# Two queue edits in a one-core attention/pooling block: low parts of weights ahead of sums and forms on VectorE, and one more panel in the last attention-branch run

## The chip, the cores and the metric

The kernel runs on one core of a Trainium2 chip. The metric is the device time of one execution in microseconds (us). Two programs that differ by less than about 0.2% can't be told apart by this kernel's measurement; the three runs below lie within 0.07%.

## The reference

One layer on 512 tokens of width 2048, all in float32. The parts that matter here, cut from the reference:

```python
h = rms_norm(x, norm_mix)
z = h @ w_in                                    # q, k, v, u, gate_a, gate_b
y_a = chunked_rel_attention(q, k, v, rel_bias)  # width 1024
y_b = multiscale_pool(u, pool_w, pool_scale)    # width 1024
merged = sigmoid(gate_a) * (y_a @ w_branch_a) + sigmoid(gate_b) * (y_b @ w_branch_b)
x = x + merged @ w_out
x = x + swiglu(rms_norm(x, norm_ffn), w_gate_up, w_down)
return rms_norm(x, norm_final)
```

## The kernel before

**Split numbers.** A float32 matmul is made of three matmuls of a reduced float32 form (fp32r). Each operand is split into a high part (a copy that rounds, on ScalarE) and a low part (the operand minus its high part, on VectorE); TensorE adds low x high, high x high and high x low in the same bank of its accumulator memory.

**First part: panels.** `panel` multiplies a panel of 256 weight columns with all tokens. Weights come in *staged units* (512 KB `raw` loads; `hi` and `lo` are their parts). A *gate panel* ("g") takes the 2048 rows of `w_in`, a *branch panel* ("y") the 1024 rows of `w_branch_a` or `w_branch_b`, so a branch panel has 2 staged units of 24 matmuls for each of two output columns. `a_order` lists the last 16 panels: g0, y0, g1, y1, ... and then, for the last `N_TAIL` values of i, all gate panels ahead of all branch panels. A branch panel's results (`m_dram`, two tiles of 128 columns for each panel) go to memory by GpSimd's queue.

**Second part: jobs.** The output projection, the gate/up projection and the down projection run as 38 *jobs*. A job takes a 1024 x 1024 block of weights and computes it by a scheme with 7 products in place of 8 (P1, P5, P6, P3, P7, P2, P4, in this order). Each product has two *units* of 12 matmuls (128 x 512), so a job has 14 units (the last two jobs, with half the rows, 7 each); I number units through all jobs (job 21 begins with unit 294) and call a unit by its number, its weight parts `hiw303`, `low303`. Three things feed a job:

- *Weights.* Quarter blocks `r11`, `r12`, `r21`, `r22` are loaded by SyncE's queue (`load2_to`). For P5, P6, P7 and P4 VectorE first adds one quarter to another in place (`t_to`, lines 842 to 848: the *running sums*). Then ScalarE makes the high part `hiw` (`hi2_to`, line 856) and VectorE the low part `low` (`lo2_to`, line 864). There are `SPLIT` = 3 buffers of each, so the parts of unit i+3 may only be written when unit i is done.
- *Forms.* The activations' side of each product ("forms", `fP1` to `fP7`, each with a high and a low part) is made from a block of 512 activations, `half`. `build_forms` is a generator, one product for each step; for four products (P5, P6, P3, P7) VectorE first makes a sum `s` (the *make*, lines 729 to 732), then ScalarE the high part (line 737), and in the next step VectorE the low part (line 740 or 742):

```python
for p, src, sign, make in plan:
    if make:
        make()
    hi, lo = forms[p][:, prs, 0], forms[p][:, prs, 1]
    nc.scalar.activation(hi, src, AF.Copy, scale=float(sign))
    yield
    if sign > 0:
        tt(lo, src, hi.bitcast(F32), op=ALU.subtract)
```

- *Results.* At the end of a product ScalarE copies an accumulator (lines 899, 904, 909) or VectorE adds one to an *output sum* (lines 911, 916, 922, 926). In gate/up jobs of the second half, `hidden` turns results into the next activations: ScalarE's Silu (line 1017, waits for an output sum), VectorE's product (line 1020), and transposes on TensorE.

**What sets the order.** Every engine works off its own queue in the order in which the Python code issues. `step()` runs all active generators (forms, `hidden`, attention) by one step; panels call it after each output column of a staged unit, jobs after each unit. `run_job` issues for unit i: the running sum of unit i+3, `hiw` of unit i+2, the 12 matmuls, the product's end if there is one, `step()`, and last `low` of unit i+2. After the last branch panel `drain()` calls `step()` until no generator is left; the forms of the first job (`build_merged(fo, 0)`) start behind the last gate panel and need `m_dram` 0 to 7, of branch panels 0 to 3, only.

Of the kernel before, what the change touches and what calls it, by code (L numbers as in the profile page):

```python
# [28 lines left out]
SPLIT = 3  # L29
# [8 lines left out]
N_C = 6  # L38
LOAD_AHEAD = 7
PAD_CONST, PAD_CONST1, PAD_SLOTS, PAD_RIGHT = 96, 56, 80, 120  # L40
N_TAIL = 3

T_BY_DMA = False

# [2 lines left out]
def hybrid_block_kernel(  # L47
# [81 lines left out]
    def add_panel(w, nk, c0, r0=0, cuts=None):  # L129
        k = 0  # L130
        for n in cuts or [KU] * (nk // KU):
            units.append((rows(w, r0 + k * P, n, c0, CU), n))
            k += n
        assert k == nk
# [4 lines left out]
    def staged(kind, i, dt=F32R):  # L139
        return stage.tile([P, KU * CU], dt, tag=kind, name=f"{kind}{i}", bufs=AHEAD if kind == "raw" else SPLIT)  # L140
# [49 lines left out]
    def step():  # L190
        now, later[:] = list(later), []
        for fn in now:
            fn()
        since[0] += 1
        if waiting and since[0] >= spacing[0]:
            active.append(waiting.popleft())
            since[0] = 0
        for g in list(active):
            if next(g, "end") == "end":
                active.remove(g)  # L200
        for n in behind:
            lo_to(n)
            load_to(n + AHEAD)
        behind.clear()
# [60 lines left out]
    for what, i in b_order:  # L265
        if what == "g":
            add_panel(w_in, KD, GB + i * CU)
        else:
            add_panel(w_branch_b, KB, i * CU)
    a_order = [x for i in range(n_blk - N_TAIL) for x in (("g", i), ("y", i))]  # L270
    a_order += [(what, i) for what in "gy" for i in range(n_blk - N_TAIL, n_blk)]
    for what, i in a_order:
# [482 lines left out]
    def ctile():  # L755
        serial[0] += 1
        return cpools[-1].tile([P, 2, 512], F32, tag="c", name=f"c_{serial[0]}")

    def bank2(kind):
        serial[0] += 1  # L760
        if kind == "a":
            return ps2.tile([P, 512], F32, tag="a", name=f"psa_{serial[0]}", bufs=2)
        return ps2.tile([P, 2, 512], F32, tag=kind, name=f"ps{kind}_{serial[0]}", bufs=2 if kind == "x" else 1)
# [49 lines left out]
    def wide(t):  # L813
        return t.rearrange("p (k c) -> p k c", c=512)

    def load2_to(n):
        while loads and loads[0][0] <= n:
            _, j, q, h = loads.pop(0)
            t = rawtile(j, q, h)
            s, f = {"11": (0, 0), "12": (0, 1), "21": (1, 0), "22": (1, 1), "t1": (0, 0), "t3": (1, 1)}[q]  # L820
            nc.sync.dma_start(wide(t), j.quarter(s, f, h))
            if q[0] == "t":
                nc.gpsimd.dma_start(wide(t), j.quarter(0, 1, h), accum_op=ALU.add)
# [3 lines left out]
    def source(i):  # L827
        j, p, h = wunits[i]
        a = ("t1" if T_BY_DMA else "11") if p in ("P5", "P6") else "11"
        q = {"P1": "11", "P5": a, "P6": a, "P3": "22", "P7": "t3" if T_BY_DMA else "12", "P2": "21", "P4": "21"}[p]  # L830
        return j.raw[q, h]

    def t_to(n):

        while st2["t"] < min(n, len(wunits)):
            i = st2["t"]
            j, p, h = wunits[i]
            r = {q: t for (q, hh), t in j.raw.items() if hh == h}
            run = r.get("t1", r.get("11"))
            lo2_to(i - j.nh + 1)  # L840
            if p == "P5" and not T_BY_DMA:
                nc.vector.tensor_tensor(run, run, r["12"], op=ALU.add)
            elif p == "P6":
                nc.vector.tensor_tensor(run, run, r["22"], op=ALU.add)
            elif p == "P7" and not T_BY_DMA:
                nc.vector.tensor_tensor(r["12"], r["12"], r["22"], op=ALU.add)
            elif p == "P4":
                nc.vector.tensor_tensor(r["21"], r["21"], run, op=ALU.add)
            st2["t"] += 1

    def hi2_to(n):
        while st2["hi"] < min(n, len(wunits)):
            i = st2["hi"]
            t_to(i + 1)
            hi_t[-1 - i] = staged("hi", f"w{i}")
            nc.scalar.activation(hi_t[-1 - i], source(i), AF.Copy)  # L856
            st2["hi"] += 1

    def lo2_to(n):
        while st2["lo"] < min(n, len(wunits)):  # L860
            i = st2["lo"]
            hi2_to(i + 1)
            lo_t[-1 - i] = staged("lo", f"w{i}")
            nc.vector.tensor_tensor(lo_t[-1 - i], source(i), hi_t[-1 - i].bitcast(F32), op=ALU.subtract)  # L864
            st2["lo"] += 1
# [3 lines left out]
    def run_job(j):  # L869
        forms = j.forms  # L870
        X = Y = Z = None
        a = p5 = u2 = None
        for n, p in enumerate(PRODUCTS):
            if p == "P1":
                X = ps = bank2("x")
            elif p == "P5":
                Y = ps = bank2("y")
            elif p == "P2":
                Z = ps = bank2("y")
            else:  # L880
                ps = Y if p == "P3" else X
            for h in range(j.nh):
                i = j.base + n * j.nh + h
                load2_to(i + LOAD_AHEAD)
                t_to(i + SPLIT + 1)
                hi2_to(i + SPLIT)
                hi, lo = wide(hi_t.pop(-1 - i)), wide(lo_t.pop(-1 - i))
                for t in range(2):
                    for k in range(2):
                        fh, fl = forms[p][:, 2 * h + k, 0, TOK[t]], forms[p][:, 2 * h + k, 1, TOK[t]]  # L890
                        first = p in ("P1", "P5", "P2") and h == 0 and k == 0
                        last = h == j.nh - 1 and k == 1
                        mm(ps[:, t], fh, lo[:, k], start=first, stop=False, skip_group_check=True)  # L893
                        mm(ps[:, t], fh, hi[:, k], start=False, stop=False, skip_group_check=True)  # L894
                        mm(ps[:, t], fl, hi[:, k], start=False, stop=last, skip_group_check=True)  # L895
                if h == j.nh - 1:
                    if p == "P1":
                        a = ctile()
                        nc.scalar.activation(a, X, AF.Copy)
                        if j.acc:  # L900
                            nc.gpsimd.dma_start(a, j.acc["11"], accum_op=ALU.add)
                    elif p == "P5":
                        p5 = ctile()
                        nc.scalar.activation(p5, Y, AF.Copy, scale=-1.0)
                        if j.acc:
                            nc.gpsimd.dma_start(p5, j.acc["22"], accum_op=ALU.add)
                    elif p == "P6":
                        u2 = ctile()
                        nc.scalar.activation(u2, X, AF.Copy, scale=-1.0)
                    elif p == "P3":  # L910
                        nc.vector.tensor_tensor(u2, u2, Y, op=ALU.subtract)
                        if j.acc:
                            nc.gpsimd.dma_start(u2, j.acc["12"], accum_op=ALU.add)
                        j.done("12", u2)
                    elif p == "P7":
                        nc.vector.tensor_tensor(p5, p5, X, op=ALU.subtract)
                        j.done("22", p5)
                        if j.acc:
                            c21 = ctile()
                            nc.sync.dma_start(c21, j.acc["21"])  # L920
                    elif p == "P2":
                        nc.vector.tensor_tensor(a, a, Z, op=ALU.add)
                        j.done("11", a)
                    elif p == "P4":
                        if j.acc:
                            nc.vector.tensor_tensor(c21, c21, X, op=ALU.add)
                        else:
                            c21 = ctile()
                            nc.scalar.activation(c21, X, AF.Copy)
                        j.done("21", c21)  # L930
                step()
                lo2_to(i + SPLIT)


    def tok2(ap, th, c0):
# [279 lines left out]
```

## Time and profile before

| | us |
|---|---|
| median of 3 runs | 2540.54 (2540.34 to 2541.96) |
| the profiled execution | 2541.46 |
| its span, first to last instruction | 2539.5 |
| TensorE busy with matmuls | 2455.2 (97%) |
| VectorE busy | 1732.6 (68%) |
| ScalarE busy | 1163.4 (46%) |
| GpSimd busy | 151.3 (6%) |
| mean granted TensorE clock | 0.992 |

The profiled execution's time is 2.0 us longer than its span. A busy share is a mean over the whole span: an engine with 68% can still be the one that is waited for in one stage.

### The profile page before, as it was taken

What the parts mean: (1) busy time and instruction counts of PE and PEld (TensorE: products, weight loads), DVE (VectorE), ACT (ScalarE), POOL (GpSimd) and SP (SyncE); (2) the same over time, 40 slices, a digit from 0 to 9 for tenths busy, and PEclk for the clock granted to TensorE, in tenths of its full rate; (3) what the DMA queues carried; (4) which work ended last, traced back from release to release, by engine and by line L of the source; (5) the groups of instructions that cost most, each with busy time, mean ns of one, the idle gap of its engine ahead of it and who ended that gap; (6) DMA issues with size and microseconds to landing.
All of it is one profiled execution on the core that took longest, in us unless ns stands there. A gap on an engine that the chain in (4) does not pass through costs nothing.

```text
span 2539.5 us, 29049 instructions
## 1 busy us (share of the span) xinstructions
PE 2455.2 (97%) x11221; PEld 2002.9 (79%) x11221; DVE 1732.6 (68%) x1996; ACT 1163.4 (46%) x1499; POOL 151.3 (6%) x242
## 2 busy tenths in 40 slices
PE   9999999999999998999999999999999999999995
PEld 7888888888888887777788888877878778787773
DVE  6445556533343327978877777888897888879885
ACT  5444443322232224466545445555554555555554
POOL 0000000000000000110000000000000001000014
PEclk9999999999999999999999999999999999999997
DMA  5322222323333336664443543645645646637374
GB/s 175 96 86 78 86 92 85 94 92 100 94 101 115 107 106 199 187 211 136 179 163 141 195 156 146 203 117 167 161 145 144 171 133 165 182 104 203 100 214 118
DMA packets 203146, 352.20 MB, mean 139 GB/s; under 512 B 11304, under 2 KB 95856, under 8 KB 202880
## 3 DMA queue, kind: packets, MB, share of 16 engines
q1 hardware_dynamic: 177760, 263.76, 30.9%
q0 software_dynamic: 24096, 84.49, 14.2%
q8 instruction: 88, 1.44, 0.2%
q10 hardware_dynamic: 1152, 2.10, 0.2%
q14 instruction: 50, 0.41, 0.0%
HBM read 289.44 MB, written 60.86 MB: 138 GB/s over the span
## 4 chain that ended last, share of the span: by engine, by line
PE 86%; DVE 8%; issue 3%; ACT 2%; DMA 1%; ACTq 0%; SPq 0%; POOL 0%; DVEq 0%; POOLq 0%
PE psd L211 10%; PE psd L212 10%; PE psd L213 10%; PE psx L893 8%; PE psx L894 8%; PE psx L895 8%; PE psy L893 7%; PE psy L895 7%; PE psy L894 7%; DVE low L864 3%; PE psd L423 1%; DVE fP L740 1%; PE psd L425 1%; PE psd L424 1%; ACT hiw L856 1%
## 5 line engine op out<-in xcount | busy, mean ns | idle before, releaser
L864 DVE TENSOR_TENSOR low<-r,hiw 128x1024 fp32r<-128x1024 f32 x518 | 630.4, 1225 | 133.7 <-ACT hiw L856 131.4
L856 ACT ACTIVATE hiw<-r 128x1024 fp32r<-128x1024 f32 x518 | 546.5, 1057 | 377.0 <-PE psx L895 157.6
L893 PE MATMUL psx<-low,fP 128*128 128x512 f32 x1184 | 471.7, 398 | 29.7 <-DVE low L864 25.2
L894 PE MATMUL psx<-hiw,fP 128*128 128x512 f32 x1184 | 463.3, 391 | 0.0
L895 PE MATMUL psx<-hiw,fP 128*128 128x512 f32 x1184 | 463.1, 391 | 0.0
L168 DVE TENSOR_TENSOR lo<-raw,hi 128x1024 fp32r<-128x1024 f32 (+1 forms) x161 | 195.9, 1218 | 322.8 <-ACT hi L159 322.6
L893 PE MATMUL psy<-low,fP 128*128 128x512 f32 x888 | 353.1, 398 | 23.9 <-DVE low L864 21.8
L159 ACT ACTIVATE hi<-raw 128x1024 fp32r<-128x1024 f32 (+1 forms) x161 | 169.2, 1053 | 427.5 <-PE psd L213 309.7
L895 PE MATMUL psy<-hiw,fP 128*128 128x512 f32 x888 | 348.3, 392 | 0.0
L894 PE MATMUL psy<-hiw,fP 128*128 128x512 f32 x888 | 348.1, 392 | 0.0
L211 PE MATMUL psd<-xh,lo 128*128 128x512 f32 x864 | 341.5, 395 | 0.0
L213 PE MATMUL psd<-xl,hi 128*128 128x512 f32 x864 | 336.7, 390 | 0.0
L212 PE MATMUL psd<-xh,hi 128*128 128x512 f32 x864 | 336.6, 390 | 0.0
L893 PEld LDWEIGHTS psx<-low,fP 128*128 128x128 f32 x1184 | 222.9, 188 | 103.5 <-DVE low L864 55.4
L895 PEld LDWEIGHTS psx<-hiw,fP 128*128 128x128 f32 x1184 | 223.1, 188 | 48.1
L894 PEld LDWEIGHTS psx<-hiw,fP 128*128 128x128 f32 x1184 | 223.1, 188 | 42.3
L893 PEld LDWEIGHTS psy<-low,fP 128*128 128x128 f32 x888 | 168.1, 189 | 68.4 <-DVE low L864 29.0
L895 PEld LDWEIGHTS psy<-hiw,fP 128*128 128x128 f32 x888 | 168.1, 189 | 36.1
L894 PEld LDWEIGHTS psy<-hiw,fP 128*128 128x128 f32 x888 | 168.5, 190 | 32.9
L211 PEld LDWEIGHTS psd<-xh,lo 128*128 128x128 f32 x864 | 162.2, 188 | 36.3 <-issue 2.4
L213 PEld LDWEIGHTS psd<-xl,hi 128*128 128x128 f32 x864 | 162.2, 188 | 34.3
L212 PEld LDWEIGHTS psd<-xh,hi 128*128 128x128 f32 x864 | 162.4, 188 | 31.9
(207 smaller groups left out, 2810.7 us busy)
## 6 DMA issues: line engine op xcount, KB each, us to landing
r<-in_w_gate_up SPq DMA_DIRECT2D x176, 512.0 KB, 7.6
raw<-in_w_in SPq DMA_DIRECT2D x127, 512.0 KB, 3.6
r<-in_w_down SPq DMA_DIRECT2D x88, 512.0 KB, 6.5
x1d<-c POOLq DMA_DIRECT2D x48, 512.0 KB, 8.0
gp<-c POOLq DMA_DIRECT2D x44, 512.0 KB, 6.0
c<-gp POOLq DMA_DIRECT2D x33, 512.0 KB, 5.2
r<-in_w_out SPq DMA_DIRECT2D x32, 512.0 KB, 9.2
raw<-in_w_branch_b SPq DMA_DIRECT2D x16, 512.0 KB, 3.3
```

The costliest lines, as they stand in the source:

```text
L159: nc.scalar.activation(hi_t[i][:, :m], raw_t[i][:, :m], AF.Copy)
L168: nc.vector.tensor_tensor(lo_t[i][:, :m], raw_t[i][:, :m], hi_t[i].bitcast(F32)[:, :m], op=ALU.subtract)
L211: mm(ps, wl, ah, start=start, stop=False)
L212: mm(ps, wh, ah, start=False, stop=False)
L213: mm(ps, wh, al, start=False, stop=stop)
L423: mm(o, XH[kk][:, tok], hi[:, k], start=first, stop=False, skip_group_check=True)
L424: mm(o, XH[kk][:, tok], lo[:, k], start=False, stop=False, skip_group_check=True)
L856: nc.scalar.activation(hi_t[-1 - i], source(i), AF.Copy)
L864: nc.vector.tensor_tensor(lo_t[-1 - i], source(i), hi_t[-1 - i].bitcast(F32), op=ALU.subtract)
L893: mm(ps[:, t], fh, lo[:, k], start=first, stop=False, skip_group_check=True)
L894: mm(ps[:, t], fh, hi[:, k], start=False, stop=False, skip_group_check=True)
L895: mm(ps[:, t], fl, hi[:, k], start=False, stop=last, skip_group_check=True)
```

## The change

`low` of unit i+2 is issued ahead of unit i's matmuls in place of behind `step()`, so on VectorE it stands ahead of the output sum of unit i and of what the generators issue in that step. `N_TAIL` goes from 3 to 4, so the order ends g4, g5, g6, g7, y4, y5, y6, y7.

```diff
-N_TAIL = 3
+N_TAIL = 4
...
                 load2_to(i + LOAD_AHEAD)
                 t_to(i + SPLIT + 1)
                 hi2_to(i + SPLIT)
+                lo2_to(i + SPLIT)
                 hi, lo = wide(hi_t.pop(-1 - i)), wide(lo_t.pop(-1 - i))
...
                 step()
-                lo2_to(i + SPLIT)
```

In what follows line numbers are those of the kernel before; behind line 887 the changed kernel's are higher by one until the old place of `lo2_to`.

VectorE, the middle of job 21 (units 301 to 304), before; `fP5`, `fP6`, ... are forms, `s` the makes, `c` the output sums:

```order
L911 TENSOR_TENSOR c_1028_13822<-c_1028_13822,psy_1021_13732 128x1024
L740 TENSOR_TENSOR fP5_1001_13404<-s_1029_13825,fP5_1001_13404 128x2x256
L730 TENSOR_TENSOR s_1029_13825<-s_1029_13825,half_1019_13723 128x512
L864 TENSOR_TENSOR low303_13871<-r12_1014_13606,hiw303_13852 128x1024
L742 SCALAR_TENSOR_TENSOR fP6_1001_13405<-s_1029_13825,fP6_1001_13405 128x2x256
L731 TENSOR_TENSOR s_1029_13825<-s_1029_13825,half_1019_13723 128x512
L864 TENSOR_TENSOR low304_13892<-r21_1023_13756,hiw304_13875 128x1024
L848 TENSOR_TENSOR r21_1023_13756<-r21_1023_13756,r11_1009_13544 128x1024
L916 TENSOR_TENSOR c_1024_13772<-c_1024_13772,psx_1017_13686 128x1024
```

The same place now:

```order
L864 TENSOR_TENSOR low303_13854<-r12_1014_13606,hiw303_13852 128x1024
L912 TENSOR_TENSOR c_1028_13824<-c_1028_13824,psy_1021_13732 128x1024
L740 TENSOR_TENSOR fP5_1001_13406<-s_1029_13827,fP5_1001_13406 128x2x256
L730 TENSOR_TENSOR s_1029_13827<-s_1029_13827,half_1019_13725 128x512
L864 TENSOR_TENSOR low304_13877<-r21_1023_13756,hiw304_13875 128x1024
L742 SCALAR_TENSOR_TENSOR fP6_1001_13407<-s_1029_13827,fP6_1001_13407 128x2x256
L731 TENSOR_TENSOR s_1029_13827<-s_1029_13827,half_1019_13725 128x512
L848 TENSOR_TENSOR r21_1023_13756<-r21_1023_13756,r11_1009_13544 128x1024
L864 TENSOR_TENSOR low305_13899<-r21_1026_13783,hiw305_13897 128x1024
L917 TENSOR_TENSOR c_1024_13774<-c_1024_13774,psx_1017_13686 128x1024
```

Each `low` has moved ahead by an output sum (where there is one) and by the two form instructions of a step; `low304` now stands directly behind the make of line 730. ScalarE's order has not changed; there, in the same units, the high part of a form and the high part of a weight alternate:

```order
L737 ACTIVATE fP5_1001_13406<-s_1029_13827 128x2x256
L856 ACTIVATE hiw303_13852<-r12_1014_13606 128x1024
L737 ACTIVATE fP6_1001_13407<-s_1029_13827 128x2x256
L856 ACTIVATE hiw304_13875<-r21_1023_13756 128x1024
L737 ACTIVATE fP3_1001_13408<-s_1029_13827 128x2x256
L856 ACTIVATE hiw305_13897<-r21_1026_13783 128x1024
```

VectorE, from the last output sums of the last branch panel (lines 664 and 665) to the first job's third unit, before:

```order
L665 TENSOR_TENSOR sg_633_7318<-sg_571_5718,sg_633_7318 128x512
L864 TENSOR_TENSOR low1_7576<-r11_643_7498,hiw1_7574 128x1024
L742 SCALAR_TENSOR_TENSOR fP6_634_7330<-s_646_7533,fP6_634_7330 128x2x256
L731 TENSOR_TENSOR s_646_7533<-s_646_7533,half_638_7372 128x512
L740 TENSOR_TENSOR fP3_634_7331<-s_646_7533,fP3_634_7331 128x2x256
L732 TENSOR_TENSOR s3_646_7534<-half_638_7372 128x512
L740 TENSOR_TENSOR fP7_634_7332<-s3_646_7534,fP7_634_7332 128x2x256
L740 TENSOR_TENSOR fP2_634_7333<-half_638_7372,fP2_634_7333 128x2x256
L740 TENSOR_TENSOR fP4_634_7334<-half_638_7372,fP4_634_7334 128x2x256
L842 TENSOR_TENSOR r11_642_7496<-r11_642_7496,r12_647_7605 128x1024
L842 TENSOR_TENSOR r11_643_7498<-r11_643_7498,r12_648_7607 128x1024
L864 TENSOR_TENSOR low2_7642<-r11_642_7496,hiw2_7616 128x1024
```

and now:

```order
L665 TENSOR_TENSOR sg_631_7248<-sg_571_5718,sg_631_7248 128x512
L864 TENSOR_TENSOR low1_7586<-r11_644_7510,hiw1_7584 128x1024
L740 TENSOR_TENSOR fP4_632_7264<-half_636_7302,fP4_632_7264 128x2x256
L842 TENSOR_TENSOR r11_643_7508<-r11_643_7508,r12_647_7605 128x1024
L842 TENSOR_TENSOR r11_644_7510<-r11_644_7510,r12_648_7607 128x1024
L864 TENSOR_TENSOR low2_7618<-r11_643_7508,hiw2_7616 128x1024
```

Six of the seven form instructions behind the last panel have moved up among the branch panels, which now call `step()` 16 times behind the last gate panel in place of 12.

## Rows read from the trace of the kernel before

**Rows 1.** The page: busy time and share of the span of each engine.

```profile
PE 2455.2 (97%) x11221; PEld 2002.9 (79%) x11221; DVE 1732.6 (68%) x1996; ACT 1163.4 (46%) x1499; POOL 151.3 (6%) x242
```

**Rows 2.** TensorE's waits: who waited for whom, total us, times, longest.

```profile
PE psx L893 <- DVE low L864: 25.2, 34, 1.5
PE psy L893 <- DVE low L864: 21.8, 13, 6.5
```

**Rows 3.** Stretches: length, then each engine's busy us, clock, DMA share, GB/s.

```profile
985.00:1060.00 75.00, 64.96 (x263) 50.09 (x262) 67.65 (x74) 38.78 (x47) 9.39 (x11) 0.95 0.71 203
...
1115.00:1235.00 120.00, 109.43 (x485) 85.02 (x484) 104.69 (x117) 81.43 (x136) 7.50 (x12) 0.99 0.48 163
1235.00:1640.00 405.00, 405.00 (x1788) 332.79 (x1787) 314.92 (x267) 197.01 (x192) 23.96 (x43) 1.00 0.48 171
1640.00:2425.00 785.00, 756.21 (x3358) 608.23 (x3357) 673.22 (x650) 428.94 (x494) 55.43 (x65) 1.00 0.54 150
2425.00:2539.50 114.50, 83.70 (x341) 66.29 (x339) 75.16 (x76) 55.53 (x80) 32.59 (x28) 0.88 0.60 157
```

**Rows 4.** VectorE in order of time behind the last panel: start, us, instruction.

```profile
990.81 0.69 DVE L742 SCALAR_TENSOR_TENSOR fP<-s,fP 128x512 fp32r<-128x512 f32 x1
...
996.73 2.35 DVE L842 TENSOR_TENSOR r<-r,r 128x1024 f32<-128x1024 f32 x2
999.15 1.23 DVE L864 TENSOR_TENSOR low<-r,hiw 128x1024 fp32r<-128x1024 f32 x1
```

**Rows 5.** The chain that ended last, 999 to 1007 us: start, us, what.

```profile
1001.23 0.43 PE psy L894
...
1006.51 0.23 PE psy L895
```

**Rows 6.** SyncE's queue behind 986 us: three loads of weight quarters.

```profile
986.40 1.73 SPq L821 DMA_DIRECT2D r<-in_w_out  x3
```

**Rows 7.** Tile `r`, 985 to 990 us: from issue to landing, us.

```profile
DMA to landing us min/median/max: 4.1/5.2/6.2
```

**Rows 8.** VectorE in job 21, units 301 to 303.

```profile
1871.46 1.22 DVE L911 TENSOR_TENSOR c<-c,psy 128x1024 f32<-128x1024 f32 x1 [0.94 <-PE psy L895]
1872.60 0.69 DVE L740 TENSOR_TENSOR fP<-s,fP 128x512 fp32r<-128x512 f32 x1
1873.32 0.69 DVE L730 TENSOR_TENSOR s<-s,half 128x512 f32<-128x512 f32 x1
1873.93 1.22 DVE L864 TENSOR_TENSOR low<-r,hiw 128x1024 fp32r<-128x1024 f32 x1
...
1877.65 1.23 DVE L848 TENSOR_TENSOR r<-r,r 128x1024 f32<-128x1024 f32 x1
```

**Rows 9.** ScalarE at the same place.

```profile
1874.05 0.63 ACT L737 ACTIVATE fP<-s 128x512 fp32r<-128x512 f32 x1 [3.05 <-DVE s L730]
1874.59 1.04 ACT L856 ACTIVATE hiw<-r 128x1024 fp32r<-128x1024 f32 x1
```

**Rows 10.** ScalarE's groups, 1115 to 2425 us: count, busy us, mean ns, idle before.

```profile
L1017 ACT ACTIVATE c<-c,r 128x512 f32<-128x512 f32 x44 | 29.4, 717 | 50.2 <-DVE c L926 33.4 <-DVE c L922 16.7
```

**Rows 11.** TensorE: first matmuls of units 289, 300, 310, one in the last job.

```profile
1832.52 0.50 PE L893 MATMUL psx<-low,fP 128*128 128x512 f32 x1 [0.33 <-DVE low L864]
...
1865.82 0.39 PE L893 MATMUL psy<-low,fP 128*128 128x512 f32 x1
...
1898.30 0.48 PE L893 MATMUL psy<-low,fP 128*128 128x512 f32 x1
...
2483.73 0.55 PE L893 MATMUL psx<-low,fP 128*128 128x512 f32 x1 [2.03 <-DVE c L916]
```

**Rows 12.** VectorE's group of the first make: count, busy us, mean ns, idle before.

```profile
L729 DVE TENSOR_TENSOR s<-half 128x512 f32<-128x512 f32 x19 | 13.0, 686 | 0.0
```

**Rows 13.** Two short stretches, each with one wait of TensorE; columns as in rows 3.

```profile
1041.00:1046.00 5.00, 3.54 (x16) 2.59 (x15) 4.96 (x7) 3.16 (x4) 0.53 (x1) 1.00 1.00 388
...
2481.00:2488.00 7.00, 4.97 (x16) 3.63 (x15) 3.77 (x3) 2.28 (x5) 3.21 (x2) 0.76 0.37 68
```

## Prediction

> **What bounds the kernel now.** The busy shares come first [rows 1]: TensorE has 97%, so only its gaps can be won. TensorE's own waits come next [rows 2]: 47 us of them end with a `low`, 34 times before a product in `psx` and 13 times in `psy`, and no other wait is near. Where these lie, the stretches show [rows 3]. From 1235 to 1640 us (the 11 gate/up jobs of the first half, no forms, no `hidden`) TensorE is busy for all of 405.0 us: 405 us over 1788 matmuls is 0.2265 us for each, so a unit of 12 takes 2.72 us, the pace against which I count. The idle time is in the stretches that build forms: 10.0 us of 75 behind the panels, 10.6 of 120 under output jobs 2 and 3 and the job behind them, 28.8 of 785 where `hidden` and forms run between jobs. In these VectorE is busy for 90, 87 and 86%. The last stretch loses 30.8 us, most of it behind the last matmul. VectorE is thus close to being the bound wherever forms are built; whether the new order helps hangs on whether it keeps VectorE as busy as it is.
>
> **Edit 1, `N_TAIL`.** Building the first job's forms takes 17 steps. Three branch panels give 12; the other five run behind the last matmul, and the VectorE rows show them: from 990.8 us to the running sums at 996.7, then `low2` until 1000.4 [rows 4]. TensorE, done with unit 1 at 994.0, waits 6.5 us for it, the longest wait of [rows 2], and starts unit 2 right behind `low2`. The chain then shows matmuls at 0.43 us until they go at 0.23 [rows 5]: 14 matmuls at the lower of the clock's two levels, 14 x 0.2 = 2.8 us lost.
> With four branch panels 16 steps run under matmuls, and one form instruction stays ahead of the running sums. So 5.9 us of VectorE's queue (990.8 to 996.7) shrink to 0.6: sums from 991.4, `hiw2` to 993.6, `low2` to 994.8, unit 2 at 994.9 in place of 1000.4: 5.5 us. Three things could be late next. The second running sum (at 992.5) needs the quarter issued first in [rows 6], at 986.4, and such loads land after 4.1 to 6.2 us [rows 7], so 990.5 to 992.6: in time. The next loads land by 994.0, before their sums. TensorE's remaining idle time is 1.2 us; idle times of 1.5 us leave the clock alone (below), so the 2.8 us come back too. Gain: 8.3 us; if the landing were late enough to leave a wait of 3 us, only 3.5 and no clock.
> The forms that move up cost VectorE some 4 us in each branch panel of 10.9 us; their queue there also holds two low parts and four sums (5.2 us), so the cover holds.
>
> **Edit 2, `low` first.** What it should give is the 47 us less the 6.5 of edit 1. At a product's end `low` of unit i+2 now stands behind the output sum (which waits for unit i) and two form instructions, and VectorE's rows show the price: sum 1.22, form 0.69, make 0.69, `low` 1.22, ending at 1875.15 [rows 8]. That is 3.7 us behind the sum's start, which was the end of unit 301, and unit 302 lasts 2.72: unit 303 waits 1.0 us. Moved ahead, that `low` no longer waits for unit i.
> But it needs `hiw`, and the order lists put a new wait there. On ScalarE `hiw304` stands behind the high part of form P6, which needs the make of line 730. ScalarE's rows give the times: form 0.63, the next starts 0.54 behind it, `hiw` 1.04 [rows 9]; from the make's end at 1874.01 to `hiw304`'s end at 1875.63 are 1.62 us. Before, VectorE filled them with `low303` and two form instructions. Now `low304` stands directly behind the make, so VectorE stands still for 1.67 us, and everything behind it too: the form instructions, and with them the next make. One step becomes a loop: low 1.22, (sum 1.14), form 0.61, make 0.7, hand-over and ScalarE 1.67: 4.2 us without an output sum, 5.3 with one, against 2.72 us for TensorE. A running sum in between (1.23, [rows 8]) only fills part of the 1.67. Each build has four makes, so four turns of the loop.
> The Trainium skill says the same of the queues, in "PSUM — Partial Sum Buffer", section "Engine vs sequencer instructions": "ScalarE/VectorE/GpSimdE queues are strict FIFO." The trace agrees: nothing in [rows 8] starts out of the order list. By a queue that let ready form instructions pass, the sum would be edit 1 and most of the 47 us.
>
> *Worked through, job 21* (unit 300 starts at 0, durations of rows 8 and 9). `hiw302` ends at 3.2, `low302` at 4.4, form and make at 5.6, `hiw303` at 7.3, `low303` at 8.5; unit 303 was due at 8.2: 0.4 late. Output sum, form and make to 11.0, `hiw304` 12.6, `low304` 13.9, due 11.4: 2.5. Form, make to 15.2, `hiw305` 16.8, `low305` 18.1, due 16.8: 1.4. Output sum, form, make to 20.5, `hiw306` 22.1, `low306` 23.4, due 21.0: 2.4. Then `low308` waits in the same way for `hiw308` behind the Silu pair of line 1017 (2 x 0.72, [rows 10]) behind an output sum: 1.0 late, unit 309 0.7, unit 310 1.5. Unit 310 starts at 38.4. Before, it started 1898.30 - 1865.82 = 32.5 behind unit 300 [rows 11]. So +5.9 us.
>
> The same by hand for the other places:
> - job 20 and its like, where the build falls into units 1 to 7 and only one output sum: waits of 0.6, 1.4, 1.3 and 0.3, so 3.6 in place of 0.6 (0.33 idle in [rows 11] and 0.3 until the pace is back): +3.0.
> - the two builds under job 0: 12.5 us above the pace in place of 5.1: +7.4.
> - `hidden` alone (the Silu pair ahead of `hiw296`): +0.5.
> - the last job's units are single, and there `t_to` has already issued each `low` ahead of the sums; the order lists differ there by two or three rows: 0. Jobs without forms had no wait and have none: 0.
>
> Counting: line 729 runs 19 times [rows 12], 2 in edit 1, so 17 builds: 7 like job 21 (6 with a `hidden` behind: 6 x 5.9 = 35.4; one without: 3), 4 like job 20 (12), 2 under job 0 (7.4), 4 under output jobs. These last I put at 12: as under job 0 (2 x 7.4), less what transposes give, which stretch TensorE's pace there. `hidden` alone 5 x 0.5 = 2.5. Edit 2 costs 35.4 + 3 + 12 + 7.4 + 12 + 2.5 = 72 us.
>
> **Bounds.** The clock: waits of 2.4 us are new here. A wait of 1.46 us within 1041 to 1046 left it at 1.00; one of 2.03 [rows 11] was followed by 0.76 over 7 us [rows 13], some 3.4 us at the lower level, 1.7 us lost. Where VectorE's loop is the bound, a slower TensorE hides under it, so I take 0 and, as the upper end, 1.7 for each of 14 such places, two for each build like job 21: +24. The lower end: if VectorE comes into each build with more lead than I gave it (one unit, 2.72 us, for 15 of the 17 builds), edit 2 costs 72 - 41 = 31.
>
> **Sum.** 2541.46 - 8.3 + 72 = 2605 us for the profiled execution; the median of the runs is 0.9 us lower: 2604. Bounds: 2541 - 8 + 31 = 2564 and 2604 + 24 = 2628.
>
> **Rivals.**
> - *The low parts come early and nothing else matters* (faster). This needs makes that run so far ahead that `hiw` never waits for a form. For it: VectorE idles 10 to 14% of these stretches. Against it: a make can't run ahead of the `low` in front of it, which waits for unit i-1 by its buffer. If so: 2541 - 8 - 41 = 2492, or with half of the waits left 2512. It decides if the loop takes under 2.72 us, where the rows say 4.2.
> - *Both effects cancel*: what the sums no longer delay equals what the makes now do. In job 21 the trace has 4.8 us of loss now (32.5 - 27.7, with one set of transposes); it would have to stay there. Then edit 1 alone is left: 2533, or 2541 if its landing is late too.
> - *The lock costs half* (more lead): 2564 to 2580, slower still, inside the range.
>
> **Chances.** Slower as forecast, 2564 to 2628: 0.80, and beyond 2628 another 0.03. Cancelling 0.09: of it 0.04 within 0.2% (5 us, about what a measurement of this kernel can tell from no change) and 0.05 faster. The faster rival 0.08. Faster 0.13, same 0.04, slower 0.83. The range 2562 to 2630 leaves out 0.18.
>
> **What would show it.** Right: in job 21 and its like VectorE has gaps of some 1.7 us ahead of `low`, put down to `hiw`, and ScalarE's `hiw` waits for makes; TensorE's waits for `low` grow from 47 to above 90 us, in the stretches of builds alone; 1235 to 1640 stays full; unit 2 starts about 1 us behind unit 1. Wrong: `low` ready before TensorE asks in units 303 to 306, or the clock lower over long stretches.

## The result, and the profile after

The changed kernel takes 2616.15 us (median of 4 runs, 2614.79 to 2616.57) where the kernel before takes 2540.86 in the same comparison: a ratio of 1.0295, 95% interval 1.0277 to 1.0313. I had forecast 2604, and slower with a chance of 0.83. The profiled execution's span is 2614.3 us, 74.8 more than before.

The page of the changed kernel, its first part and the group at the head of the fifth:

```profile
PE 2475.1 (95%) x11221; PEld 2019.3 (77%) x11221; DVE 1736.9 (66%) x1996; ACT 1159.5 (44%) x1499; POOL 151.1 (6%) x242
...
L864 DVE TENSOR_TENSOR low<-r,hiw 128x1024 fp32r<-128x1024 f32 x518 | 635.9, 1228 | 302.3 <-ACT hiw L856 300.3
```

The busy times of VectorE and ScalarE are those of [rows 1] within 5 us: no work was added. What grew is VectorE's idle time ahead of `low`. The same group in the kernel before:

```profile
L864 DVE TENSOR_TENSOR low<-r,hiw 128x1024 fp32r<-128x1024 f32 x518 | 630.4, 1225 | 133.7 <-ACT hiw L856 131.4 <-PE psy L895 1.3
```

VectorE now stands 300 us for `hiw` in place of 131. TensorE's waits after, in the columns of [rows 2]:

```profile
PE psy L894 <- DVE low L864: 53.3, 36, 2.6
PE psx L894 <- DVE low L864: 42.6, 40, 2.3
PE psa L953 <- ACT half L962: 11.3, 4, 6.5
```

The waits for `low` have gone from 47 to 96 us, in 76 places in place of 47, and the long one of 6.5 us is not among them: the 6.5 us that is left is another, at the transposes. By stretch, shifted with the program against [rows 3]:

```profile
985.00:1060.00 75.00, 64.71 (x266) 49.70 (x265) 63.58 (x68) 35.73 (x42) 9.39 (x11) 0.98 0.68 203
1115.00:1255.00 140.00, 113.32 (x468) 87.38 (x468) 99.15 (x113) 79.47 (x133) 7.50 (x12) 0.91 0.40 136
1255.00:1660.00 405.00, 405.00 (x1788) 335.37 (x1787) 317.87 (x266) 198.06 (x193) 23.95 (x43) 1.00 0.47 169
1660.00:2500.00 840.00, 772.10 (x3368) 618.65 (x3368) 677.01 (x653) 425.54 (x494) 55.44 (x65) 0.99 0.51 142
```

The jobs without forms are as full as before (405.0 of 405). The stretch with `hidden` and forms (1660 to 2500) is 55 us longer, the one under the output jobs and behind them (1115 to 1255) 20 us. In both VectorE is busy for a smaller share than before: 81% where it had 86, and 71% where it had 87.

VectorE in job 21, at the place of [rows 8]; the last column is the idle time before an instruction, and whom it waited for:

```profile
1910.58 1.23 DVE L864 TENSOR_TENSOR low<-r,hiw 128x1024 fp32r<-128x1024 f32 x1 [1.65 <-ACT hiw L856]
1911.72 1.21 DVE L912 TENSOR_TENSOR c<-c,psy 128x1024 f32<-128x1024 f32 x1
1912.85 0.68 DVE L740 TENSOR_TENSOR fP<-s,fP 128x512 fp32r<-128x512 f32 x1
1913.57 0.69 DVE L730 TENSOR_TENSOR s<-s,half 128x512 f32<-128x512 f32 x1
1915.90 1.22 DVE L864 TENSOR_TENSOR low<-r,hiw 128x1024 fp32r<-128x1024 f32 x1 [1.64 <-ACT hiw L856]
1917.05 0.68 DVE L742 SCALAR_TENSOR_TENSOR fP<-s,fP 128x512 fp32r<-128x512 f32 x1
1917.77 0.69 DVE L731 TENSOR_TENSOR s<-s,half 128x512 f32<-128x512 f32 x1
1918.37 1.22 DVE L848 TENSOR_TENSOR r<-r,r 128x1024 f32<-128x1024 f32 x1
1920.11 1.23 DVE L864 TENSOR_TENSOR low<-r,hiw 128x1024 fp32r<-128x1024 f32 x1 [0.51 <-ACT hiw L856]
```

and ScalarE there, as [rows 9]:

```profile
1914.30 0.63 ACT L737 ACTIVATE fP<-s 128x512 fp32r<-128x512 f32 x1 [3.75 <-DVE s L730]
1914.83 1.04 ACT L856 ACTIVATE hiw<-r 128x1024 fp32r<-128x1024 f32 x1
```

This is the loop of the prediction, which I call a *turn* each time it comes round: the make of line 730 ends at 1914.26, ScalarE's form starts 0.04 us later, `hiw` behind it ends at 1915.87, and only then `low` starts. From one such `low` to the next are 5.3 us with an output sum between them, the figure of the prediction. Where a running sum (line 848) stands between make and `low`, the stop is 0.51.

Edit 1 shows in TensorE's row for unit 2, and job 21 in those for units 300 and 310 [rows 11]:

```profile
994.70 0.50 PE L894 MATMUL psy<-low,fP 128*128 128x512 f32 x1 [1.16 <-DVE low L864]
...
1903.29 0.39 PE L894 MATMUL psy<-low,fP 128*128 128x512 f32 x1
...
1941.37 0.47 PE L894 MATMUL psy<-low,fP 128*128 128x512 f32 x1 [1.35 <-DVE low L864]
```

Unit 2 was forecast at 994.9 with a wait of 1.2 us. Unit 310 starts 38.1 us behind unit 300, forecast at 38.4.

### The profile page after: what moved, and what is told of

Its sections match the earlier page's. It is cut to its first block, busy times and chain, and to the rows that moved or that the text cites. A ratio compares the mean times of both kernels' runs of the same rounds, so it can differ in the third digit from the quotient of the medians.

```text
span 2614.3 us, 29069 instructions
## 1 busy us (share of the span) xinstructions
PE 2475.1 (95%) x11221; PEld 2019.3 (77%) x11221; DVE 1736.9 (66%) x1996; ACT 1159.5 (44%) x1499; POOL 151.1 (6%) x242
## 4 chain that ended last, share of the span: by engine, by line
PE 71%; DVE 11%; issue 9%; ACT 6%; DMA 1%; POOL 0%; ACTq 0%; SPq 0%; DVEq 0%; POOLq 0%
PE psd L211 8%; PE psd L213 8%; PE psd L212 8%; PE psx L894 7%; PE psx L895 7%; PE psx L896 7%; PE psy L894 6%; PE psy L896 6%; PE psy L895 6%; DVE low L864 4%; ACT hiw L856 4%; PE psd L423 1%; DVE fP L740 1%; PE psd L425 1%; PE psd L424 1%
## 5 line engine op out<-in xcount | busy, mean ns | idle before, releaser
L864 DVE TENSOR_TENSOR low<-r,hiw 128x1024 fp32r<-128x1024 f32 x518 | 635.9, 1228 | 302.3 <-ACT hiw L856 300.3
L896 PEld LDWEIGHTS psx<-hiw,fP 128*128 128x128 f32 x1184 | 225.8, 191 | 49.1
L895 PEld LDWEIGHTS psx<-hiw,fP 128*128 128x128 f32 x1184 | 226.3, 191 | 44.8
L895 PEld LDWEIGHTS psy<-hiw,fP 128*128 128x128 f32 x888 | 168.9, 190 | 33.6
```

## Experiments

The theory is the **lock**: the loss comes from `low` standing behind a make for whose product's high part `hiw` waits. The rivals: displaced output sums, VectorE simply full, the four branch panels. All times are medians in us, against runs of the kernel before on the same chip; "the fast run" in two expectations is `e4_low_after_forms`.

| kernel | time | before | ratio (95%) | VectorE idle for `hiw` |
|---|---|---|---|---|
| changed kernel | 2616.15 | 2540.86 | 1.0295 (1.0277 to 1.0313) | 300.3 |
| e1_tail_alone | 2533.12 | 2541.24 | 0.997 (0.9959 to 0.998) | 132.2 |
| e2_low_first_alone | 2621.40 | 2541.24 | 1.0315 (1.0299 to 1.033) | 301.1 |
| e3_low_behind_sum | 2579.71 | 2540.37 | 1.0153 (1.0138 to 1.0168) | 213.8 |
| e4_low_after_forms | 2501.47 | 2541.24 | 0.9845 (0.9831 to 0.9858) | 179.6 |
| e5_make_one_step_ahead | 2527.96 | 2541.24 | 0.9948 (0.9936 to 0.9961) | 203.0 |
| e6_make_ahead_old_low | 2536.98 | 2540.37 | 0.9985 (0.9976 to 0.9995) | 126.2 |
| e7_low_after_forms_make_ahead | 2493.67 | 2540.63 | 0.9814 (0.9798 to 0.9831) | 156.9 |
| e8_low_first_outside_builds | 2532.06 | 2540.37 | 0.9967 (0.9954 to 0.998) | 185.9 |
| e9_low_first_end_behind_step | 2572.69 | 2540.37 | 1.0127 (1.011 to 1.0143) | 258.7 |
| e10_low_last_end_behind_step | 2517.25 | 2540.63 | 0.9903 (0.9888 to 0.9918) | 125.5 |
| e11_two_makes_ahead | 2546.44 | 2540.63 | 1.0022 (1.0013 to 1.0031) | 235.8 |
| e12_squares_behind_copies | 2615.66 | 2540.63 | 1.0294 (1.0279 to 1.0309) | 298.9 |

The last column alone does not give the time: where VectorE stands with lead to spare, as in jobs without forms, it costs nothing. So I also read where the time is lost. For each unit I took the start of its first matmul in both traces; what the difference to the kernel before grows by, from the first unit named to the second, is what a place costs (us):

| units | what is there | changed | e2 | e3 | e9 | e11 | e5 | e4 |
|---|---|---|---|---|---|---|---|---|
| to 3 | end of the panels | -8.2 | -0.4 | -7.7 | -9.0 | -8.1 | -8.7 | -7.6 |
| 3 to 16 | 2 builds under job 0 | +7.7 | +7.4 | +4.8 | +7.8 | +0.3 | -1.2 | -0.9 |
| 44 to 74 | 4 builds: 2 begin in the last output job (job 3), 2 in job 4 | +23.4 | +22.5 | +15.2 | +22.8 | +4.0 | -2.1 | -0.2 |
| 280 to 290 | 1 build, one output sum | +3.0 | +3.0 | +3.1 | +4.7 | -0.7 | -0.7 | -0.7 |
| 300 to 310 | 1 build, then `hidden` (job 21) | +5.6 | +5.6 | +2.3 | +0.5 | +1.9 | +0.6 | -2.2 |
| to 517 | all | +74.7 | +80.4 | +38.6 | +30.1 | +6.5 | -13.4 | -40.2 |

### Each edit alone

e1 is the kernel before and e2 the changed kernel, each with one line of the other:

```diff
e1, the kernel before:
-N_TAIL = 3
+N_TAIL = 4
e2, the changed kernel:
-N_TAIL = 4
+N_TAIL = 3
```

> Edit 1 alone: N_TAIL is 4, the low parts stay at their old place. Lock theory (the loss of the change comes from the low part standing right behind a form's make on VectorE): the lock is not there, only edit 1's gain is left, 2541 - 8.3 = 2532.5 us (2530 to 2536); TensorE's waits for low parts fall from 47 to about 41 us, unit 2 starts about 1 us behind unit 1. Rival (the four branch panels in a row cost something of their own, and are part of the 75 us): 2545 us or more.

> Edit 2 alone: N_TAIL stays 3, the low parts stand ahead of sums and forms. Lock theory: all of the loss and none of edit 1's gain, 2616 + 8 = 2624 us (2621 to 2628). Rival (part of the loss is that the first job meets another order behind four branch panels): under 2612 us.

Edit 1 alone gives 8.1 us, edit 2 alone costs 80.2; together that is 72.1, where the change costs 75.3. The two add up to within some 3 us, and the four panels cost nothing of their own. In e1 TensorE's waits for `low` are 44 us, 3 more than I said.

### The lock, broken with `low` still first

```diff
e5, the changed kernel:
-                ("P6", s, -1, lambda: tt(s, s, a11, op=ALU.add)),
-                ("P3", s, 1, lambda: tt(s, s, a12, op=ALU.subtract)),
+                ("P6", s3, -1, lambda: tt(s3, s, a11, op=ALU.add)),
+                ("P3", s, 1, lambda: tt(s, s3, a12, op=ALU.subtract)),
...
-        for p, src, sign, make in plan:
-            if make:
-                make()
+        for n, (p, src, sign, _) in enumerate(plan):
+            if n + 1 < len(plan) and plan[n + 1][3]:
+                plan[n + 1][3]()
```

> The changed kernel (low first, N_TAIL 4) with every make of a form issued one step earlier than its high part; the makes alternate between the two tiles s and s3. Order of low parts, sums and forms otherwise as in the changed kernel. Lock theory: when a low part is reached, the make that its weight's high part waits for is one step old, so the stop of 1.7 us goes, and what is left is low parts that wait neither for sums nor for makes: 2541 - 8 - 28 = 2505 us (2490 to 2528), with TensorE's waits for low parts under 30 us in place of 96. Rival (displaced sums and form instructions, or VectorE too full in these stretches): nothing of that is changed, 2590 to 2616 us.

2527.96: the makes alone take 88 us off the changed kernel, with every `low`, sum and form where the change put it. At the place in job 21 VectorE then reads:

```profile
1859.24 0.69 DVE L730 TENSOR_TENSOR s<-s,half 128x512 f32<-128x512 f32 x1
1859.84 1.22 DVE L864 TENSOR_TENSOR low<-r,hiw 128x1024 fp32r<-128x1024 f32 x1
1860.98 1.21 DVE L912 TENSOR_TENSOR c<-c,psy 128x1024 f32<-128x1024 f32 x1
1862.11 0.68 DVE L740 TENSOR_TENSOR fP<-s,fP 128x512 fp32r<-128x512 f32 x1
1862.83 0.69 DVE L731 TENSOR_TENSOR s<-s,half 128x512 f32<-128x512 f32 x1
1863.44 1.22 DVE L864 TENSOR_TENSOR low<-r,hiw 128x1024 fp32r<-128x1024 f32 x1
```

There is no idle time ahead of either `low`. But the run is 23 us above my 2505, and TensorE's waits for `low` are 44 us, not under 30: against edit 1 alone low-first without the lock is worth 5 us. Two things stand in the place of the lock. In these units VectorE works without a break (in this trace it stands for less than 0.1 us from 1856.4 to 1875.7), and `low308` behind them waits for `hiw308`, which stands on ScalarE behind a Silu pair that waits for an output sum. So by this trace VectorE's own work and the Silu pair are next in line; no run tried either by itself.

> Control for the run with makes one step ahead: the same makes one step ahead, N_TAIL 4, but the low parts at their old place behind the form step. Lock theory: there was no lock to break in the old order, so within 6 us of edit 1 alone, 2527 to 2539 us; the 88 us that the early makes gave in the changed kernel belong to the order with low first alone. Rival (early makes help VectorE by themselves): under 2515 us.

The control: with `low` at its old place the early makes change 2533.12 to 2536.98, 4 us slower. By themselves they give nothing; they are worth 88 us where `low` stands first.

### Half of the makes

The diff is that of e5, with `make()` called one step early for P6 and P7 only: in the steps of P5 and P3 VectorE issues two makes, the step's own and the next.

> The changed kernel with two of the four makes of a build (P6 and P7) issued one step early, so that two turns of the lock are left in each build. All four early gave 88 us. Lock theory: the loss goes by the turn, so half of it, 2616 - 44 = 2572 us (2555 to 2590). Rival (the loss is a matter of VectorE's fullness, which makes in pairs leave as it is): 2600 us or more.

2546: 70 of the 88 us, where I expected half. VectorE's rows in job 21 show why:

```profile
1870.63 0.69 DVE L729 TENSOR_TENSOR s<-half 128x512 f32<-128x512 f32 x1
1871.35 0.69 DVE L730 TENSOR_TENSOR s<-s,half 128x512 f32<-128x512 f32 x1
1872.96 1.22 DVE L865 TENSOR_TENSOR low<-r,hiw 128x1024 fp32r<-128x1024 f32 x1 [0.92 <-ACT hiw L857]
...
1878.29 0.69 DVE L732 TENSOR_TENSOR s<-half 128x512 f32<-128x512 f32 x1
1878.90 1.22 DVE L849 TENSOR_TENSOR r<-r,r 128x1024 f32<-128x1024 f32 x1
1880.04 1.22 DVE L865 TENSOR_TENSOR low<-r,hiw 128x1024 fp32r<-128x1024 f32 x1
```

The early make stands between the step's own make and `low` and fills part of its stop: 0.92 us in place of 1.65, and none where a running sum stands there as well. My count by turns was too simple: what matters is the work between make and `low`.

### Where `low` stands against sums and forms

```diff
e3: order in each unit   matmuls, product's end, low, step()
e4:                      matmuls, step(), low, product's end
e9:                      low, matmuls, step(), product's end
e10:                     matmuls, step(), product's end, low
e8: the changed kernel   if not building[0]: lo2_to(i + SPLIT)  ahead of the matmuls,
                         lo2_to(i + SPLIT)                      behind step() in any case
```

> The changed kernel with the low part moved behind the product's end but still ahead of the form step (matmuls, output sum, low part, form step). Lock theory: in the units without an output sum the low part still stands directly behind the last step's make, so about half of the stops of 1.7 us stay, and the low parts wait for the unit's end again: 2595 us (2570 to 2616). Rival (the low parts cost because output sums stand behind them): the sums are back in front, so about edit 1 alone, 2533 us, at most 2545.

> The changed kernel (low first, N_TAIL 4), but with the product's end and its output sum behind the form step, as in the fast run with the low part behind the forms. Lock theory: the low part still stands directly behind a make, so most of the loss stays; only the stops behind the Silu pairs go, because these now start one step later: 2600 us (2580 to 2614). Rival (the fast run owes its 32 us against edit 1 to the later product's end and not to the place of the low part): 2525 us or less.

In both an output sum comes to stand between make and `low`, in the units that have one. e3 came out as the lock says (2580), not as displaced sums say. e9 fell below my range (2573, and I had put 2580 to 2614): I had not counted the sum as cover. The table of places shows it in both: in the build of units 280 to 290, with one output sum only, the loss stays in full (3.1 and 4.7), in job 21 it falls from 5.6 to 2.3 and 0.5. VectorE in e9, first in units 280 to 290, then in job 21:

```profile
1840.94 0.69 DVE L731 TENSOR_TENSOR s<-s,half 128x512 f32<-128x512 f32 x1
1844.19 1.23 DVE L864 TENSOR_TENSOR low<-r,hiw 128x1024 fp32r<-128x1024 f32 x1 [2.55 <-ACT hiw L856]
...
1892.86 0.68 DVE L729 TENSOR_TENSOR s<-half 128x512 f32<-128x512 f32 x1
1893.46 1.22 DVE L913 TENSOR_TENSOR c<-c,psy 128x1024 f32<-128x1024 f32 x1
1895.19 1.23 DVE L864 TENSOR_TENSOR low<-r,hiw 128x1024 fp32r<-128x1024 f32 x1 [0.52 <-ACT hiw L856]
```

The stop of 2.55 is longer than the others because in e9 a product's end, a copy of 1.01 us (line 906), stands on ScalarE between the form and `hiw` there.

> N_TAIL 4; the low part goes ahead of sums only in units where no build of forms is under way, in the others it stays behind the form step. Lock theory: the loss is in the builds alone, so edit 1 plus some 0.6 us for each of 5 Silu pairs that now stand ahead of a weight's high part: 2533 + 3 = 2536 us (2528 to 2544). Rival (low first costs wherever output sums are displaced): 2560 us or more.

2532, within the lock's range: outside the builds low-first costs nothing, and gives nothing that can be told from edit 1 alone.

> N_TAIL is 4; in each unit the order is matmuls, form step, low part, and last the product's end with its output sum. The low part stays ahead of the output sum, but stands behind the form instructions again, so the weight's high part that it needs stands on ScalarE ahead of the form's high part of that step. Lock theory: no stop of 1.7 us for each make, and no wait for the unit's end either, so faster than both kernels: 2541 - 8 - 20 = 2513 us (2495 to 2530). Rival (the loss comes from output sums that stand behind a low part, so that results, Silu and the next activations are late): the sums stand as late as in the changed kernel, so at least half of the loss stays, 2575 us or more.

2501, 1.5% below the kernel before; I had said 2513, and it is inside that range. Here `low` stands behind the form instructions, so the `hiw` that it needs was issued ahead of that step's form. VectorE in job 21, and ScalarE at the same place:

```profile
1853.91 0.69 DVE L730 TENSOR_TENSOR s<-s,half 128x512 f32<-128x512 f32 x1
1854.52 1.22 DVE L864 TENSOR_TENSOR low<-r,hiw 128x1024 fp32r<-128x1024 f32 x1
...
1852.10 1.06 ACT L856 ACTIVATE hiw<-r 128x1024 fp32r<-128x1024 f32 x1 [0.86 <-PE psy L895]
1854.63 0.63 ACT L737 ACTIVATE fP<-s 128x512 fp32r<-128x512 f32 x1 [1.47 <-DVE s L730]
```

The make is directly ahead of `low` again, as in the changed kernel, and VectorE does not stop: `hiw` is done at 1853.16, before the make has even begun. It is not the neighbour on VectorE that counts but the order on ScalarE, whether `hiw` is ahead of that make's form or behind it.

> N_TAIL 4; matmuls, form step, product's end with its output sum, low part last: against edit 1 alone only the product's end has moved behind the form step, against the fast run (2501 us) only the low part has moved behind the sum. If the fast run's 32 us come from low parts that no longer wait for a sum and so for the unit's end: as edit 1 alone, 2533 us (2526 to 2541). If they come from the later end (Silu pairs that stand behind one more weight's high part): 2500 to 2512 us.

2517, between the two cases: of the 32 us by which e4 beats edit 1, 16 come from the product's end behind the form step, and 16 from `low` ahead of the sum. That end puts a Silu pair one `hiw` later; that the pair's place is the whole of these 16 us was not tried by itself.

> The fast run (low part behind the form step, ahead of the product's end) with the makes one step ahead as well. Lock theory: with the low part behind the form step there is no lock left to break, 2501 us (2496 to 2507). Rival (a lock of another place is left there): under 2494 us.

2493.67, the best of all: faster than both kernels, 1.9% below the kernel before. That is 8 us below e4, where the lock theory had no change: something was left after all. By unit starts 7 of the 8 lie in units 58 to 74; there two of TensorE's waits from 1150 to 1215 us are in e4, and in e7:

```profile
PE psy L893 <- DVE low L864: 4.4, 2, 3.6
PE psa L953 <- ACT half L962: 3.0, 1, 3.0
```

```profile
PE psy L893 <- DVE low L864: 1.5, 2, 1.4
PE psa L953 <- ACT half L962: 0.6, 1, 0.6
```

With early makes ScalarE is less late there, at the copies behind the transposes and at the norm's few instructions that stand ahead of a `low`. These waits fall by 5.3 us, those for `low` ahead of `psx` grow by 0.5. A further 1.6 us lie in unit 59, behind the transposes' wait: it takes 4.77 us in e4, at a granted clock of 0.64, and 3.18 in e7, at 1.00.

### The builds under output jobs

These, the four of units 44 to 74, cost 23.4 us where I had 12. The trace offers a reason: TensorE waits up to 6.5 us at the transposes for ScalarE's copies (line 962), and ScalarE had stood 3.6 us for a make just before. In the kernel before these waits are 4.9 us in all, in the changed kernel 11.3 (below):

```profile
PE psa L953 <- ACT half L962: 4.9, 2, 3.0
```

```diff
e12, the changed kernel, x1_ready:
-        for t in range(2):
-            nc.scalar.activation(sq, c[:, t], AF.Square,
-                                 accum_out=ssq1[:, 2 * th + t, 2 * p + fb:2 * p + fb + 1])
-            yield
...
         yield from turned(c, th, halves[p, fb], lambda n: gains[:, m0 + n:m0 + n + 1])
+        for t in range(2):
+            nc.scalar.activation(sq, c[:, t], AF.Square,
+                                 accum_out=ssq1[:, 2 * th + t, 2 * p + fb:2 * p + fb + 1])
+            yield
...
-                active.append(wait_then(14, second_norm()))
+                active.append(wait_then(40, second_norm()))
```

> The changed kernel with the two squares of each block of x1 moved behind the transposes' copies on ScalarE, and the norm that reads them later. For the 23 us that the four builds under output jobs cost in place of my 12. Queue theory (ScalarE, late by the lock, comes late to the copies that free the transposes' banks, so that TensorE stands for up to 6.5 us there): less stands ahead of the copies, the 6.5 us fall by 1.4 to 4 us and the time to 2610 us (2605 to 2613). Rival (each of these builds pays the lock in full, as under later jobs, 5.9 us, and the wait at the transposes is only where it shows): 2616 us, within 2.

2615.66: no change, and the stretch costs 23.8 us against 23.4. The queue theory missed. But the edit did more than I meant: with the squares two steps go from ahead of the transposes, so TensorE comes to these two units earlier (8 each in units 54 and 55 in place of 56 and 57). TensorE's waits from 1115 to 1255 us in the changed kernel and in this one:

```profile
PE psx L894 <- DVE low L864: 13.2, 9, 2.3
PE psa L953 <- ACT half L962: 11.3, 4, 6.5
PE psy L894 <- DVE low L864: 2.0, 2, 1.3
```

```profile
PE psa L953 <- ACT half L962: 13.4, 2, 10.2
PE psx L894 <- DVE low L864: 10.7, 10, 2.3
PE psy L894 <- DVE low L864: 4.6, 3, 2.5
```

The longest wait went from 6.5 to 10.2 us, others went away, and the time stayed. That fits the rival: the transposes are where TensorE meets the lag of VectorE and ScalarE, and not its cause. It does not show it, as the transposes moved too. The rival's price fits as a mean only: 23.4 for four builds is 5.85 for each, and I had 5.9 for builds like job 21, but by unit starts the four cost 5.3, 8.9, 5.6 and 3.6 us (units 44, 53, 59, 67 and 74). Why they differ is open.

## Why the prediction was right, and where its sum was off

- **Edit 1: right.** Forecast -8.3; unit 3 starts 8.2 us earlier, e1 is 8.1 faster. Unit 2 starts 5.7 earlier (forecast 5.5), and 2.4 more come from its matmuls at the higher clock (forecast 2.8).
- **The mechanism of edit 2: right.** Stops of 1.65 us ahead of `low` (forecast 1.67), a loop of 5.3 us, `hiw` behind makes, waits for `low` at 96 us (forecast above 90), jobs without forms untouched. It is shown by e5 and e6 together (the makes one step early take 88 us off the new order and nothing off the old), by e4 (the make next to `low` costs nothing once `hiw` is ahead of its form), and by e8, which puts the whole loss into the builds.
- **Job 21 and its like: right, and not by luck.** 5.6 us each where I had 5.9 (33.6 for six). The steps came out as well: in job 16, the first of its like, the seven waits are 0.2, 2.4, 1.2, 2.2, 0.7, 0.5 and 1.4 us, where I had 0.4, 2.5, 1.4, 2.4, 1.0, 0.7 and 1.5. Job 20's like 3.0 (forecast 3.0), job 0 7.7 (7.4), `hidden` alone 0.6 (0.5).
- **"Four under output jobs ... I put at 12": too small.** They cost 23.4. The step that failed is "as under job 0 (2 x 7.4), less what transposes give": it priced a build at 3.7 us where one like job 21's costs 5.6, and took off a credit for transposes that no run shows: TensorE's waits at them grew by 6.4 us. Of the two builds under job 0 the first costs 2.3 us and the second 5.3; why the first is cheap is open.
- **"One without 3": too small.** The last such build cost 5.0 although no `hidden` follows (3.4 in e2; why the two differ is open).
- These two terms were 13.4 us too small, the other terms of edit 2 together 1.5 too large, and 1.3 us were gained outside the places that I counted (0.5 of it in the last job). By unit starts edit 2 costs 82.9 where I had 72; the median came to 2616 where I had 2604. That the miss stayed at 12 us owes a little to these opposite signs.
- **The clock: right to leave it out of builds like job 21.** My upper end had +24 for it. The changed kernel's granted clock does fall below 1.00 in builds (0.96 from 1900 to 1945 us, 0.91 from 1115 to 1255), yet unit 310 came 0.3 us earlier than my sum without a clock term. That the loop hides it is shown by jobs 16 and 21 (last section). At the transposes it is not hidden.
- **The faster rival** asked for makes that run ahead. e5 gives it just that, and at 2528 does not reach its 2492. The orders that come near (e4 2501, e7 2494) leave `low` behind the forms.
- **The order on the queues** decided the sign: in job 21 the form instruction of line 742 had its high part at 1914.93 us, but it stood behind the `low` that waited until 1915.90, and started at 1917.05. The Trainium skill says in "PSUM — Partial Sum Buffer", section "Engine vs sequencer instructions", that these engines' queues are strictly first in, first out. The trace agrees.

## What to carry to other kernels

When an instruction is moved forward on one engine's queue, follow what it waits for on the other engine, and see what stands ahead of *that*: here `low` on VectorE waited for `hiw` on ScalarE, which stood behind a form that waited for VectorE's make just ahead of `low`. Such a turn between two engines costs its hand-over (1.65 us here) each time, unless independent work stands between the two; a make one step early or the consumer behind the forms took it away, a sum in between shortened it. A long wait on TensorE may show only where a lag is met: change what it waits for, and see whether the total moves.

## What was not expected of the hardware

TensorE's longest wait is no measure of a stretch's cost: in e12 it grew from 6.5 to 10.2 us at the same total, while shorter waits around it went away.

A lower clock cost nothing in one place and its full time in another. Units 234 (job 16) and 304 (job 21) of the changed kernel both start behind a wait of 2.40 us, and the clock fell after one of them only; in the columns of [rows 3], from the start of each unit to the next:

```profile
1694.51:1698.62 4.11, 2.96 (x12) 2.14 (x13) 3.56 (x5) 1.58 (x2) 0.00 (x0) 1.00 0.26 54
...
1917.27:1921.69 4.42, 4.42 (x13) 3.47 (x14) 3.87 (x5) 1.58 (x2) 0.00 (x0) 0.61 0.33 71
```

Unit 235 then waits 1.15 us for its `low` and unit 305 not at all, and from unit 230 to 240 are 38.08 us, as from 300 to 310. There VectorE and ScalarE set the time, and the slower matmuls only fill TensorE's wait.

Unit 58 starts behind the 6.5 us at the transposes:

```profile
1189.98:1195.18 5.20, 5.20 (x18) 4.14 (x17) 1.83 (x2) 3.36 (x9) 0.00 (x0) 0.59 0.00 0
```

At a granted clock of 0.59, so mostly at the lower of the two levels (1.2 GHz), it takes 5.2 us, four transposes included; unit 59 with as many takes 3.2 at 1.00. In e2 unit 58 takes 3.9 us at 0.80, and these 1.3 us are still there at unit 62. So here the clock has its price. It is hardly a part of the change's loss, though: in the kernel before unit 58, behind a wait of 3.0 us, takes 4.8 at 0.64, which leaves 0.4 us.
